# Norm 1 of a transformer block: shift and scale as fused sums over rows of 1024, squares summed on TensorE tile by tile

## The chip, the cores and the metric

The kernel runs on one core of one Trainium2 chip. A core has a matrix engine (TensorE, called PE in the profile, with its weight loads shown apart as PEld), a vector engine (VectorE, DVE), an engine for activations (ScalarE, ACT), a general one (GpSimd, POOL) and one that here only issues DMA transfers (SyncE, SP). Each engine has its own queue and takes its instructions in order; they wait for each other through semaphores. Data lie in SBUF, 128 partitions wide; TensorE writes its sums to banks of PSUM.

The metric is the device time of one execution, in microseconds, as the median of several runs.

## The reference, cut to what matters

One layer of an encoder block on 1024 tokens with 1024 channels. The change concerns only its first lines:

```python
c_act = jax.nn.silu(c)                              # c: 1 x 1024
mod = c_act @ ada_w[l] + ada_b[l]                   # 1024 x 6144 weights
sh1, sc1, g1, sh2, sc2, g2 = split(mod, 6)
h = rmsnorm(x, ln1_g[l]) * (1.0 + sc1) + sh1        # norm 1
p = h @ w_in[l]                                     # q, k, v, gates, convolution
```

`rmsnorm` divides every token by the root of the mean square of its 1024 channels and multiplies by `ln1_g`. Shift `sh1` and scale `sc1` are two vectors of 1024 numbers, each the product of the 1024 numbers silu(c) with a 1024 x 1024 part of `ada_w`. Everything after this (attention, convolution, gates, output projection, feed-forward network) is left as it is by the change.

## The kernel before

All is float32. Large products are done as three products of split operands: an operand is split into a rounded high part (`whi`, `hh`) and the rest (`wlo`, `hl`), and high x high, high x low and low x high are summed (lines 276 and 122 to 124).

The stage in question holds x transposed: 8 tiles of 128 channels by 1024 tokens (`xt`, 512 KB each). It does the following:

1. **Squares.** As each tile k arrives, ScalarE squares its two halves of 512 tokens (line 228) and VectorE adds them to a running sum `sqa` (line 230). TensorE multiplies each tile once by ones only to be warmed up (line 232). When all tiles are there, eight one-column products with `ones` sum `sqa` over the 128 channels of a tile, one for each 128 tokens, into columns of the PSUM tile `md` (line 234). Two small instructions (line 113, `rs_m`) and a power on GpSimd (line 114) give the inverse root, which TensorE spreads over all partitions (`bcast`, line 242).
2. **Shift and scale.** For each channel tile e, 1 MB of `ada_w` arrives as 128 partitions (input channels) by 8 input tiles by 256 outputs (128 of shift, 128 of scale). `mod_sums` (lines 201 and 204) does eight multiply-adds over 256 elements on VectorE: `acc` += `ada[:, k]` * silu(c) of partition and tile k. `mod_end` sums `acc` over the partitions by two one-column products with ones (line 214), adds the bias (line 215, `mod`) and forms (1 + scale) * gain (line 216, `a1`).
3. **h and the first product.** `norm_x` multiplies a half of an x tile by the inverse root (line 258, VectorE). `make_h` applies scale and shift (line 262, ScalarE), rounds (line 263, ScalarE) and takes the rest (line 264, GpSimd). `split_wq` splits half of a weight tile (lines 187, ScalarE, and 188, GpSimd). `real` then multiplies 7 of the 8 token tiles by 512 columns of the key/value weights: 21 products for each channel tile k (line 276). The eighth token tile follows where its PSUM bank is free.

The loop over k runs 7 times: VectorE does most of `mod_sums(k + 2)`, TensorE two or three token tiles, then `mod_end(k + 1)`, ScalarE and GpSimd make h(k + 1), and TensorE does the remaining token tiles. The order inside each engine is the order of the code: `in_order` ties every instruction of an engine to the one before it, from the squares to the end of this loop. Work from later in the program may be placed between by the planner, which orders the rest of the program by an estimate of its own. After the loop come the last channel tile, then the key products over the same h (loop over `cc`), whose weights are split by ScalarE and VectorE (lines 61 and 62), while GpSimd and VectorE form sums of parts of h (`factors`, line 127) for later products.

Transfers: x, then `ada` 0, weight 0, `ada` 1, 2, weight 1, `ada` 3 are queued on SP (lines 163, 170, 176); `ada` has two buffers that share the pool `big` with the squares and with h, and three of its own, so from tile 5 on a load waits for the sums of an earlier tile. Where h takes over a buffer of `ada`, GpSimd waits for its sums. Constants come by ScalarE's queue (line 97).

Of the kernel before, what the change touches and what calls it, by code (L numbers as in the profile page):

```python
# [8 lines left out]
F32 = mybir.dt.float32  # L9
F32R = mybir.dt.float32r  # L10
AF = mybir.ActivationFunctionType
ALU = mybir.AluOpType
# [4 lines left out]
P = 128  # L17
# [12 lines left out]
def block_kernel(tc, x, x_t, cols, ada_1, ada_2, ada_row, w_q, w_kv, w_v1, w_cg, w_a, w_b, w_o, w_g, w_u, w_d, out):  # L30
# [8 lines left out]
    def nm(s):  # L39
        uid[0] += 1  # L40
        return f"{s}_{uid[0]}"
# [119 lines left out]
    adb = bigp.tile([P, 2, KT, 256], F32, tag="big", bufs=4, name=nm("adb"))  # L161
    for k in range(KT):
        nc.sync.dma_start(xt[:, k, :], x_t[k])
    wq = []
    MC0, MC, MS, NS1, NM = 3, 2, 5, 2, 2
    ads = []

    def load_ada(e):
        ad = adb[:, e] if e < 2 else sp.tile([P, KT, 256], F32, tag="ada", bufs=3, name=nm("ada"))
        nc.sync.dma_start(ad, ada_1[e])  # L170
        ads.append(ad)

# [11 lines left out]
    def split_wq(k):  # L184
        cs = slice(k % 2 * 512, k % 2 * 512 + 512)
        hi, lo = wq[k // 2]
        nc.scalar.activation(hi[:, cs], wraw[k // 2][:, cs], AF.Copy)
        nc.gpsimd.tensor_tensor(out=lo[:, cs], in0=wraw[k // 2][:, cs], in1=hi[:, cs].bitcast(F32), op=ALU.subtract)
# [4 lines left out]
        load_ada(2 * q + 1)  # L193
    a1 = const.tile([P, 8], F32, name="a1")

    def mod_sums(e):

        ad = ads[e]
        acc = sp.tile([P, 256], F32, tag="acc", bufs=2, name=nm("acc"))
        accs[e] = acc  # L200
        nc.vector.tensor_scalar(out=acc, in0=ad[:, 0, :], scalar1=ca[:, 0:1], scalar2=None, op0=ALU.mult)
        yield
        for k in range(1, KT):
            nc.vector.scalar_tensor_tensor(out=acc, in0=ad[:, k, :], scalar=ca[:, k:k + 1], in1=acc,
                                           op0=ALU.mult, op1=ALU.add)
            yield

    accs = {}

    def mod_end(e):  # L210
        acc = accs.pop(e)
        ps = md[:, 2 * e:2 * e + 2]
        for j in range(2):
            nc.tensor.matmul(ps[:, j:j + 1], acc[:, j * P:(j + 1) * P], ones[:, 0:1], start=True, stop=True)
        nc.vector.tensor_tensor(out=mod[:, 0:2, e], in0=ps, in1=acol[:, 0:2, e], op=ALU.add)
        nc.vector.scalar_tensor_tensor(out=a1[:, e:e + 1], in0=mod[:, 1, e:e + 1], scalar=1.0,
                                       in1=ln1[:, e:e + 1], op0=ALU.add, op1=ALU.mult)


    sqa = sqb[:, 0]  # L220
    ssp = md[:, 16:24]
    rsp = [ps_tr() for n in range(2)]
    warm = ps_pj()
    for k in range(KT):
        for n in range(2):
            ns = slice(n * 512, n * 512 + 512)
            sq = sqb[:, 1 + k % 3, ns] if k else sqa[:, ns]
            nc.scalar.activation(sq, xt[:, k, ns], AF.Square)
            if k:
                nc.vector.tensor_tensor(out=sqa[:, ns], in0=sq, in1=sqa[:, ns], op=ALU.add)  # L230
        if k < NWARM:
            nc.tensor.matmul(warm, ones, xt[:, k, :512], start=True, stop=True)
    for i in range(8):
        nc.tensor.matmul(ssp[:, i:i + 1], sqa[:, i * P:(i + 1) * P], ones[:, 0:1], start=True, stop=True)
    ms0 = mod_sums(0)
    for j in range(NM):
        next(ms0)
    rts = [rstd_of(ssp[:, 4 * n:4 * n + 4], 1.0 / D, sp, 4, eng=nc.vector) for n in range(2)]

    def bcast(n):  # L240
        for i in range(4):
            nc.tensor.matmul(rsp[n][:, i * P:(i + 1) * P], rts[n][:, i:i + 1].broadcast_to([P, P]), ident,
                             start=True, stop=True)
# [12 lines left out]
    def norm_x(k, n):  # L256
        src = xt[:, k, n * 512:(n + 1) * 512]
        nc.vector.tensor_tensor(out=src, in0=src, in1=rs[:, n * 512:(n + 1) * 512] if k else rsp[n], op=ALU.mult)
# [16 lines left out]
                if q in parts:  # L275
                    nc.tensor.matmul(ps, a, b, start=(k == 0 and q == 0), stop=(k == KT - 1 and q == 2))  # L276

    for _ in ms0:
        pass
    def sums(k):  # L280
        ms = mod_sums(k)
        for j in range(8):
            next(ms)
            if j in (3, 5):
                norm_x(k, j // 4)
            yield

    split_wq(0)
    bcast(0)
    ms = sums(1)  # L290
    for j in range(NS1):
        next(ms)
    norm_x(0, 0)
    mod_end(0)
    bcast(1)
    norm_x(0, 1)
    make_h(0, 0)
    for n in range(2):
        nc.scalar.activation(rs[:, n * 512:(n + 1) * 512], rsp[n], AF.Copy)
    make_h(0, 1)  # L300
    NPRE = 7
    pss = [ps_pj() for i in range(5)] + [ps_tr() for i in range(2)]

# [2 lines left out]
            for i in range(i0, i1):  # L306
                mm_tok(pss[i], i, wq, k, k + 1, parts)

    for _ in ms:
        pass  # L310
    for k in range(KT - 1):
        if k + 2 < KT:
            ms = sums(k + 2)
            for j in range(MS):
                next(ms)
        mc = MC if k else MC0
        real(k, 0, mc)
        split_wq(k + 1)
        mod_end(k + 1)
        for n in range(2):  # L320
            make_h(k + 1, n)
        real(k, mc, NPRE)
        for _ in ms:
            pass
        if k + 4 < KT:
            load_ada(k + 4)
            if k % 2 == 0:
                load_wq(k // 2 + 2)
# [1021 lines left out]
```

## Time and profile before

| | us |
|---|---|
| median of 3 runs | 1945.4 |
| lowest and highest | 1941.25, 1946.02 |
| the profiled execution, its own time | 1945.62 |
| its span in the profile | 1943.8 |
| TensorE busy | 1853.6 |
| VectorE busy | 1462.3 |
| ScalarE busy | 864.6 |
| GpSimd busy | 673.7 |
| mean granted TensorE clock | 0.986 |

In the rows of the profile, a time is in microseconds from the start of the span unless marked; "x3" counts instructions that a row puts together; "out<-in" names the tiles written and read; what stands in brackets is the idle time of the engine before the row and the instruction that ended it. A row of waits gives the waiting instruction, the one waited for, the total, how often, and the longest. In the rows by stretch (start:end), the columns are the length, the busy time and number of instructions of each engine asked for, the clock granted to TensorE (1.00 is full), the mean busy share of the DMA engines, and GB/s. In rows of groups stand busy time in us, mean of one in ns, and the idle time before them. L204 is line 204 of the kernel.

### The profile page before, as it was taken

The numbers are of one execution on the slowest core, as the hardware profiler recorded it, in microseconds if no ns is written. First come the engines' busy times: TensorE is split into PE (matmuls) and PEld (weight loads), VectorE is DVE, ScalarE is ACT, GpSimd is POOL, SyncE is SP. The second block draws the span as 40 slices with busy tenths as digits, with TensorE's granted clock in tenths as the row PEclk, the third lists the DMA queues.
The fourth block names the chain that finished last, engine by engine and source line by source line (L and its number), as shares of the span: only waits on it lengthen the run. The fifth ranks groups of instructions, "written<-read, shape, count | busy, mean of one in ns | idle before, by whom it ended". The sixth has DMA issues, their size and how long they took to land.

```text
span 1943.8 us, 25154 instructions
## 1 busy us (share of the span) xinstructions
PE 1853.6 (95%) x8869; PEld 1519.5 (78%) x8869; DVE 1462.3 (75%) x1927; ACT 864.6 (44%) x1597; POOL 673.7 (35%) x475
## 2 busy tenths in 40 slices
PE   7899999998999999998999999979999999999899
PEld 4678767777888888887888788867888888878587
DVE  8865687778664799998999644499988788743854
ACT  4442343223333677776777421464444434422221
POOL 3694547978231001111000000065454444301713
PEclk8899999999999999999999999999999999999999
DMA  6465544334445756559554535323343334399566
GB/s 276 162 208 172 190 154 160 136 114 152 170 171 197 214 158 189 169 167 302 161 161 128 189 130 193 133 82 136 146 173 152 141 143 171 119 347 321 218 221 224
DMA packets 151149, 347.47 MB, mean 179 GB/s; under 512 B 15088, under 2 KB 52208, under 8 KB 149104
## 3 DMA queue, kind: packets, MB, share of 16 engines
q1 hardware_dynamic: 74000, 218.80, 34.4%
q10 hardware_dynamic: 76016, 123.40, 17.6%
q0 software_dynamic: 1008, 3.67, 0.5%
q8 instruction: 70, 1.15, 0.2%
q14 instruction: 55, 0.45, 0.1%
HBM read 235.19 MB, written 110.62 MB: 178 GB/s over the span
## 4 chain that ended last, share of the span: by engine, by line
PE 43%; DVE 10%; issue 3%; DMA 3%; ACT 2%; POOL 1%; ACTq 0%; SPq 0%; DVEq 0%; POOLq 0%
PE e L122 6%; PE e L124 6%; PE e L123 6%; PE e L1203 3%; PE e L1204 3%; PE e L1202 3%; PE pj L785 3%; PE pj L786 3%; PE pj L787 3%; DVE pt L710 2%; DVE wlo L965 2%; PE e L1020 1%; PE e L1022 1%; PE e L1021 1%; PE tr L726 1%
## 5 line engine op out<-in xcount | busy, mean ns | idle before, releaser
L710 DVE TENSOR_TENSOR_SCAN pt<-pt,dm 128x256 f32<-128x256 f32 (+7 forms) x128 | 173.9, 1363 | 5.3 <-ACT pt L705 5.1
L123 PE MATMUL e<-big,whi 128*128 128x512 f32 x352 | 138.0, 392 | 7.8 <-DVE big L127 7.8
L122 PE MATMUL e<-big,whi 128*128 128x512 f32 x352 | 137.7, 392 | 0.8 <-ACT c L1118 0.8
L124 PE MATMUL e<-big,wlo 128*128 128x512 f32 x352 | 137.5, 391 | 0.0
L1203 PE MATMUL e<-wlo,f 128*128 128x512 f32 (+1 forms) x319 | 123.1, 386 | 9.5 <-DVE wlo L965 9.5
L124 PE MATMUL pj<-big,wlo 128*128 128x512 f32 x320 | 127.0, 398 | 5.1 <-DVE wlo L127 5.1
L113 POOL TENSOR_SCALAR rs_m<-ss 128x1 f32<-128x1 f32 x8 | 2.0, 245 | 365.3 <-ACT xn L1035 365.3
L122 PE MATMUL pj<-big,whi 128*128 128x512 f32 x320 | 128.0, 400 | 0.4 <-ACT whi L438 0.4
L276 PE MATMUL pj<-whi,big 128*128 128x512 f32 x352 | 116.3, 410 | 11.6 <-ACT big L263 8.9
L123 PE MATMUL pj<-big,whi 128*128 128x512 f32 x320 | 127.1, 397 | 0.0
L705 ACT ACTIVATE pt<-z,rq 128x512 f32<-128x512 f32 (+2 forms) x192 | 112.3, 587 | 30.5 <-PE z L704 17.6
L1204 PE MATMUL e<-whi,f 128*128 128x512 f32 (+1 forms) x319 | 121.8, 382 | 0.0
L1202 PE MATMUL e<-whi,f 128*128 128x512 f32 (+1 forms) x319 | 118.5, 383 | 2.0 <-ACT fs L1142 1.4
L127 DVE TENSOR_TENSOR c<-e,c 128x512 f32<-128x512 f32 x154 | 102.8, 681 | 21.1 <-PE e L124 21.1
L829 POOL TENSOR_TENSOR ybl<-cy,ybh 128x512 fp32r<-128x512 f32 x16 | 29.0, 1810 | 255.7 <-ACT ybh L828 242.9
L438 ACT ACTIVATE whi<-raw 128x512 fp32r<-128x512 f32 x116 | 72.7, 633 | 94.4 <-PE pj L123 32.6
L706 ACT ACTIVATE sg<-z,rq 128x512 f32<-128x512 f32 (+1 forms) x192 | 112.7, 590 | 1.3 <-DVE mb L851 1.3
L127 DVE TENSOR_TENSOR c<-pj,c 128x512 f32<-128x512 f32 x140 | 93.2, 681 | 24.3 <-PE pj L124 24.1
L127 DVE TENSOR_TENSOR wlo<-ws,whi 128x512 fp32r<-128x512 f32 x80 | 73.6, 939 | 50.0 <-ACT whi L438 49.8
L730 DVE TENSOR_TENSOR atl<-tr,ath 128x512 fp32r<-128x512 f32 (+1 forms) x192 | 100.3, 544 | 10.7 <-ACT ath L729 10.3
L127 POOL TENSOR_TENSOR ws<-raw,raw 128x512 f32<-128x512 f32 x41 | 57.9, 1412 | 144.1 <-DMA raw<-w_cg 80.7
L729 ACT ACTIVATE ath<-tr 128x512 fp32r<-128x512 f32 (+1 forms) x192 | 90.4, 498 | 37.8 <-PE tr L726 12.7
(250 smaller groups left out, 5641.9 us busy)
## 6 DMA issues: line engine op xcount, KB each, us to landing
f<-d_f SPq DMA_DIRECT2D x77, 512.0 KB, 4.4
d_f<-fs ACTq DMA_DIRECT2D x70, 512.0 KB, 2.6
raw<-w_cg SPq DMA_DIRECT2D x40, 512.0 KB, 3.4
mada<-ada ACTq DMA_DIRECT2D x32, 512.0 KB, 4.2
raw<-w_g SPq DMA_DIRECT2D x24, 512.0 KB, 3.2
raw<-w_u SPq DMA_DIRECT2D x23, 512.0 KB, 3.2
d_k<-khl ACTq DMA_DIRECT2D x32, 256.0 KB, 2.2
d_q<-gt ACTq DMA_DIRECT2D x32, 256.0 KB, 2.1
```

The lines of the kernel that those rows point to most:

```text
L122: nc.tensor.matmul(ps, wh[:, k, :], fh[:, k, :], start=(k == 0), stop=False)
L123: nc.tensor.matmul(ps, wh[:, k, :], fl[:, k, :], start=False, stop=False)
L124: nc.tensor.matmul(ps, wl[:, k, :], fh[:, k, :], start=False, stop=(k == 3))
L127: eng.tensor_tensor(out=out, in0=a, in1=b, op=op)
L276: nc.tensor.matmul(ps, a, b, start=(k == 0 and q == 0), stop=(k == KT - 1 and q == 2))
L705: nc.scalar.activation(pt[:, off + s0:off + s0 + m], z[:, :m], AF.Sigmoid, scale=rq[:, 1, i, h:h + 1])
L706: nc.scalar.activation(sg[:, s0:s0 + m], z[:, :m], AF.Sigmoid, scale=rq[:, 0, i, h:h + 1])
L710: nc.vector.tensor_tensor_scan(out=pt[:, rev], data0=pt[:, rev], data1=dm[:, rev], initial=0.0, op0=ALU.mult, op1=ALU.add)
L730: nc.vector.tensor_tensor(out=tl[:, :nb, c0:c0 + P], in0=src, in1=th[:, :nb, c0:c0 + P].bitcast(F32), op=ALU.subtract)
L1202: nc.tensor.matmul(o, sh, w[0][:, c], start=(j == 0), stop=False)
L1203: nc.tensor.matmul(o, sh, w[1][:, c], start=False, stop=False)
L1204: nc.tensor.matmul(o, sl, w[0][:, c], start=False, stop=(j == NJ - 1))
```

## The change

Two things are done in another way, and the loop is reordered.

- **Squares:** ScalarE squares the first half of each x tile and VectorE the second; there is no running sum on VectorE. TensorE sums the squares of each tile as it comes: eight one-column products for every tile, accumulated in `md` over all 8 tiles (64 in place of 8).
- **Shift and scale:** `ada_w` is laid out the other way round, with 128 output channels on the partitions and 1024 inputs in a row, for shift and for scale. silu(c) is spread over all partitions: a 512 KB broadcast transfer of c on ScalarE's queue (`cab`), a sigmoid and a product, placed after the second tile of x. One fused instruction on VectorE then multiplies a row of 1024 by `cab` and sums it (`mod_sum`); two of them, for shift and for scale, replace the eight multiply-adds and the two one-column products. Each is issued as two instructions, the product and the read of the accumulator.
- **Order:** `mod_sum`, `mod_end` and `norm_x` of tile k + 2 now follow `make_h` of k + 1 in the code, in one piece, and no longer wait for TensorE. Before the loop, the sums of tile 0 come after the `rs_m` instructions, and those of tile 1 after the norm of tile 0.

```diff
+    cab = sp.tile([P, D], F32, name="cab")
+    nc.scalar.dma_start(cab, ada_row[2:3, :].broadcast_to([P, D]))
...
+    def mod_sum(e, m):
+        if not m:
+            msum[e] = sp.tile([P, 2], F32, tag="msum", bufs=4, name=nm("msum"))
+        pr = sp.tile([P, D], F32, tag="prod", bufs=2, name=nm("prod"))
+        nc.vector.tensor_tensor_reduce(out=pr, in0=ads[e][:, m], in1=cab, scale=1.0, scalar=0.0, op0=ALU.mult,
+                                       op1=ALU.add, accum_out=msum[e][:, m:m + 1])
...
     def mod_end(e):
-        acc = accs.pop(e)
-        ps = md[:, 2 * e:2 * e + 2]
-        for j in range(2):
-            nc.tensor.matmul(ps[:, j:j + 1], acc[:, j * P:(j + 1) * P], ones[:, 0:1], start=True, stop=True)
-        nc.vector.tensor_tensor(out=mod[:, 0:2, e], in0=ps, in1=acol[:, 0:2, e], op=ALU.add)
+        nc.vector.tensor_tensor(out=mod[:, 0:2, e], in0=msum.pop(e), in1=acol[:, 0:2, e], op=ALU.add)
...
     for k in range(KT):
-        for n in range(2):
-            ns = slice(n * 512, n * 512 + 512)
-            sq = sqb[:, 1 + k % 3, ns] if k else sqa[:, ns]
-            nc.scalar.activation(sq, xt[:, k, ns], AF.Square)
-            if k:
-                nc.vector.tensor_tensor(out=sqa[:, ns], in0=sq, in1=sqa[:, ns], op=ALU.add)
+        sq = sqb[:, k % 4]
+        nc.scalar.activation(sq[:, :512], xt[:, k, :512], AF.Square)
+        nc.vector.tensor_tensor(out=sq[:, 512:], in0=xt[:, k, 512:], in1=xt[:, k, 512:], op=ALU.mult)
         if k < NWARM:
             nc.tensor.matmul(warm, ones, xt[:, k, :512], start=True, stop=True)
-    for i in range(8):
-        nc.tensor.matmul(ssp[:, i:i + 1], sqa[:, i * P:(i + 1) * P], ones[:, 0:1], start=True, stop=True)
+        for i in range(8):
+            nc.tensor.matmul(ssp[:, i:i + 1], sq[:, i * P:(i + 1) * P], ones[:, 0:1], start=(k + i == 0), stop=(k + i == KT + 6))
+        if k == 1:
+            sb = sp.tile([P, D], F32, tag="prod", bufs=2, name=nm("sb"))
+            nc.scalar.activation(sb, cab, AF.Sigmoid)
+            nc.vector.tensor_tensor(out=cab, in0=cab, in1=sb, op=ALU.mult)
...
     for k in range(KT - 1):
-        if k + 2 < KT:
-            ms = sums(k + 2)
-            for j in range(MS):
-                next(ms)
         mc = MC if k else MC0
         real(k, 0, mc)
         split_wq(k + 1)
-        mod_end(k + 1)
         for n in range(2):
             make_h(k + 1, n)
+        if k + 2 < KT:
+            for m in range(2):
+                mod_sum(k + 2, m)
+            mod_end(k + 2)
+            for n in range(2):
+                norm_x(k + 2, n)
         real(k, mc, NPRE)
```

More of the change, by code (lines that the diff above doesn't have):

```diff
@@ L276, in mm_tok @@
                     nc.tensor.matmul(ps, a, b, start=(k == 0 and q == 0), stop=(k == KT - 1 and q == 2))
[L278 to L282, printed above, removed]
-            next(ms)
-            if j in (3, 5):
-                norm_x(k, j // 4)
-            yield
     split_wq(0)
+    for m in range(2):
+        mod_sum(0, m)
+    mod_end(0)
     bcast(0)
-    ms = sums(1)
-    for j in range(NS1):
-        next(ms)
     norm_x(0, 0)
-    mod_end(0)
     bcast(1)
+    make_h(0, 0)
     norm_x(0, 1)
-    make_h(0, 0)
+    make_h(0, 1)
     for n in range(2):
         nc.scalar.activation(rs[:, n * 512:(n + 1) * 512], rsp[n], AF.Copy)
-    make_h(0, 1)
+    for m in range(2):
+        mod_sum(1, m)
+    mod_end(1)
+    for n in range(2):
+        norm_x(1, n)
     NPRE = 7
```

33 lines of the change are left out of this document (8 added, 25 removed).

## The prediction

> **What bounds the kernel now.** I read the page first, then the waits of the first 110 us, one step of the loop in order of time, and the start in order of time. The diff touches only the work before the first key/value product is done; of everything later the changed program keeps the order, but for some local swaps. So the question is when that product ends.
>
> ```profile
> span 1943.8 us, 25154 instructions
> PE 1853.6 (95%) x8869; PEld 1519.5 (78%) x8869; DVE 1462.3 (75%) x1927; ACT 864.6 (44%) x1597; POOL 673.7 (35%) x475
> ```
> ```profile
> ACT xt L262 <- DVE a L216: 36.6, 8, 7.0
> ```
> ```profile
> 43.90:51.70 7.80, 5.75 (x27) 4.20 (x26) 7.62 (x13) 3.27 (x6) 4.15 (x4) 1.00 0.75 269
> ```
> Over the kernel TensorE (PE) is the bound, but not here. The waits say that ScalarE, whose `big` TensorE multiplies, waits for `a` of VectorE (36.6 us in 8 steps). The row of one loop step (columns: PE, PEld, DVE, ACT, POOL busy) has VectorE busy 7.62 of 7.80 us. One step, in order of time:
>
> ```profile
> 43.53 2.76 POOL L264 TENSOR_TENSOR big<-xt,big 128x512 fp32r<-128x512 f32 x2 [3.65 <-ACT big L263]
> 43.77 1.38 DVE L201 TENSOR_SCALAR acc<-ada,ca 128x256 f32<-128x256 f32 x1
> ...
> 45.19 3.33 DVE L204 SCALAR_TENSOR_TENSOR acc<-ada,ca,acc 128x256 f32<-128x256 f32 x3
> 46.25 1.46 POOL L188 TENSOR_TENSOR wlo<-raw,whi 128x512 fp32r<-128x512 f32 x1
> ...
> 48.43 0.68 DVE L258 TENSOR_TENSOR xt<-xt,rs 128x512 f32<-128x512 f32 x1
> 49.03 0.48 DVE L204 SCALAR_TENSOR_TENSOR acc<-ada,ca,acc 128x256 f32<-128x256 f32 x1
> 49.43 0.15 DVE L215 TENSOR_TENSOR mod<-pj,cst 128x2 f32<-128x2 f32 x1
> ...
> 49.81 0.81 ACT L262 ACTIVATE xt<-xt,mod,a 128x512 f32<-128x512 f32 x1 [4.47 <-DVE a L216]
> ...
> 51.36 2.76 POOL L264 TENSOR_TENSOR big<-xt,big 128x512 fp32r<-128x512 f32 x2 [3.65 <-ACT big L263]
> ```
> A multiply-add takes 0.48 us alone (49.03) and 1.11 on average beside GpSimd (3.33 for 3). Each GpSimd instruction is followed by one VectorE instruction, and so on: with inputs from SBUF they take turns. A step is therefore not the sum of VectorE's own work, but of the turns of both.
>
> **The start, and what the change adds to it.** All squares of x are now summed on TensorE as each of the 8 tiles arrives: per tile the warm-up product and 8 one-column products, each as two load-and-multiply pairs (16 rows for 8 products in the profile). Before, that was done once, after 14 adds on VectorE.
>
> ```profile
> 7.16 0.34 PEld L232 LDWEIGHTS pj<-xt,ones 128*128 128x128 f32 x1 [0.52 <-DMA xt<-x_t]
> 8.02 0.34 PEld L232 LDWEIGHTS pj<-xt,ones 128*128 128x128 f32 x1 [0.52 <-issue]
> ...
> 9.46 0.19 PEld L232 LDWEIGHTS pj<-xt,ones 128*128 128x128 f32 x1 [0.25 <-issue]
> 9.89 0.19 PEld L232 LDWEIGHTS pj<-xt,ones 128*128 128x128 f32 x1 [0.24 <-issue]
> ...
> 14.77 1.86 PEld L234 LDWEIGHTS pj<-ones,sqb 128*128 128x128 f32 x16 [1.15 <-DVE sqb L230]
> ...
> 20.92 0.93 PEld L214 LDWEIGHTS pj<-ones,acc 128*128 128x128 f32 x4 [1.61 <-DVE acc L204]
> 21.73 1.83 PEld L242 LDWEIGHTS tr<-dm,rs_r 128*128 128x128 f32 x8
> ```
> ```profile
> 4.47 9.98 PE L232 MATMUL pj<-xt,ones 128*128 128x512 f32 x16 [4.47 <-DMA xt<-x_t]
> ...
> 16.76 0.23 DVE L113 TENSOR_SCALAR rs_m<-pj 128x4 f32<-128x4 f32 x2 [0.16 <-PE pj L234]
> ...
> 24.08 1.65 PE L276 MATMUL pj<-whi,big 128*128 128x512 f32 x3 [0.23 <-ACT big L263]
> ```
> A pair starts every 0.11 us at the full clock (1.86 for 16) and every 0.21 at half clock (1.83 for 8, less the tail of the last; the 4 one-column pairs at 20.92 go at the same rate). One half of the warm-up product takes 0.86 us at the start (7.16 to 8.02) and 0.43 once the clock is full (9.46 to 9.89). So a tile costs 2 x 0.855 + 16 x 0.213 = 5.12 us at half clock; at full clock both terms halve, to 0.85 + 1.78 = 2.63. In both cases this is more than the 1.2 us in which a tile of x arrives (9.98 for 8), so TensorE sets the end of this stage. Which clock it gets decides the whole change:
>
> ```profile
> 16.01:19.42 3.41, 1.79 (x15) 1.00 1.04 438
> 19.42:22.83 3.41, 1.99 (x10) 0.50 1.01 423
> ...
> 50.14:53.56 3.42, 1.87 (x8) 1.00 0.48 134
> 53.56:56.97 3.41, 3.41 (x19) 1.00 0.92 257
> ...
> 60.38:63.79 3.41, 3.05 (x10) 0.50 0.48 204
> 63.79:67.21 3.42, 3.42 (x9) 0.50 0.44 153
> 67.21:70.60 3.39, 3.39 (x18) 1.00 0.00 0
> ```
> ```profile
> 60.75 1.22 PE L276 MATMUL pj<-whi,big 128*128 128x512 f32 x2 [0.36 <-POOL big L264]
> 61.77 0.85 PE L214 MATMUL pj<-ones,acc 128*128 128x1 f32 x4
> 62.48 1.63 PE L276 MATMUL pj<-whi,big 128*128 128x512 f32 x3
> ```
> These are stretches of TensorE (busy us, count, granted clock), cut where the clock changes, every 3.41 us. The stretch from 60.38 is busy for 3.05 of 3.41 us and the next one is still at half clock; only after 63.79 to 67.21, all of it wide products, is the clock full. What the first lacks is columns: five products of 512 columns at some 0.43 us (1.63 for 3, less the tail of the last) are 2.1 us, 62%; the four one-column pairs fill time but stream nothing. In the same way 1.79 us of narrow work (from 16.01) loses the clock and 1.87 us of mostly wide work (from 50.14) keeps it. In the new start the streaming share is 1.71 of 5.12 us, and at most 1.71 of any 3.41, 50%. So I take half clock to the end of the stage: 4.47 + 8 x 5.12 = 45.4, and `rs_m` at 45.6 in place of 16.76: **+28.8 us**.
>
> The Trainium skill's page TensorE: Matmul & The Clock Gate (section Why this matters for your kernels) advises to keep TensorE busy for at least 4 us without a gap to get the full clock. Taken by queue occupancy, that rule would let this stage run at full clock, for the result of the second rival below; the 60.38 row does not agree with it so read.
>
> Hidden in this stage: the second half of each square, moved to VectorE (8 x 0.68 in place of 14 adds); the sigmoid and the product for `cab` (about 1.6 us on ScalarE, twice the 0.81 of a pass over 512, and as much on VectorE); the 512 KB broadcast, issued on ScalarE's queue ahead of its squares, which takes x's transfers some 1.2 us at the 420 to 440 GB/s of the rows above. Their cover is TensorE's 5.1 us a tile; without it they cost at most their own time. SP's queue keeps its order; the five `ada` tiles that have a buffer, with x and three weights some 11 MB, need 26 us at that rate and are there. The later three wait for a sum to free a buffer, as before, and have three steps to land.
>
> **The loop.** Removed per step: 8 multiply-add instructions and 4 one-column pairs with the wait of `mod` for TensorE. Added: 2 fused sums over 1024 with a read of the accumulator each. No row has this instruction. Bounds, by nearest rows of 1024 elements from SBUF:
>
> ```profile
> L710 DVE TENSOR_TENSOR_SCAN pt<-pt,dm 128x1024 f32<-128x1024 f32 x16 | 36.5, 2279 | 0.6 <-ACT pt L705 0.5
> ...
> L712 DVE TENSOR_TENSOR sg<-sg,pt 128x1024 f32<-128x1024 f32 x16 | 19.8, 1240 | 0.1
> ```
> ```profile
> 29.34 1.27 POOL L264 TENSOR_TENSOR big<-xt,big 128x512 fp32r<-128x512 f32 x1 [3.97 <-DVE acc L204]
> ```
> The plain product, 1.24 us, is the lower end (it must stream the same elements); the scan, 2.28, the upper, since it also carries a value along the row. A sum needs no value for each element before the next product, so I take 1.24, plus 0.1 for the read (the small `mod` above takes 0.15, overlapped).
>
> The Trainium skill's Vector Engine (DVE) Microarchitecture Reference (section 7, Points that are easy to get wrong) says that two-source instructions with accumulator run at half rate when both sources are SBUF and wider than bf16. That would be the upper end, and the first rival's result; no row here shows such an instruction, only that the multiply-add without accumulator does not (256 elements in 0.48).
>
> Turns per step: GpSimd 3 x 1.27 = 3.8; VectorE 2 x 1.1 + 2 x 0.53 (the streaming parts of 1.24 and 0.68) = 3.3; together **7.1 us** in place of 7.85 (43.53 to the like place at 51.36). VectorE's own work, 4.3 us, would allow less, but turns are taken in order. `mod` and `a` now both have two sources in SBUF and wait for a turn; they are short and fall between.
>
> From `rs_m`: itself 0.2, two sums 2.7, a turn of GpSimd 1.3, `mod` and `a` 0.3, the norm 0.7, ScalarE's two passes 0.8 + 0.6: first product at +6.7 (before: 24.08 - 16.76 = 7.3). Step 0 runs at half clock for most of its 24 products at 0.427 and takes 8; then 6 steps of 7.1; the last h at +57.
>
> ```profile
> 84.90:95.80 10.90, 10.90 (x49) 1.00 0.38 118
> ```
> ```profile
> 85.10 6.01 POOL L127 TENSOR_TENSOR tb<-big,big 128x512 f32<-128x512 f32 x4
> ```
> Then TensorE alone: 39 products at 0.227 us (this row: 10.9 for 48 or so), 8.9 us: the product ends at +65.8. Before, it ended at 95.85 (the last of its 192 products is at the end of that row), 79.1 after `rs_m`. Gain **-13.3**. The eighth token tile may start early, as the bank `md` is free; that moves 7 of its 24 products into TensorE's gaps and is in the 39.
>
> After it, the fourth weight of the next product is split on VectorE behind two factor instructions that need six GpSimd instructions after the last `hl`. At 1.5 us each (6.01 for 4) or a little more these end near +69, the split near +71; TensorE wants it at 65.8 + 18 x 0.227 = +69.9. I take **+1** (bounds 0 and 2.5); before, GpSimd's last `hl` was 10.7 us ahead of the product's end (85.10), now some 7.
>
> Sum: 28.8 - 13.3 + 1 = +16.5 on 1945.6, the profiled execution's own time (its span 1943.8 and 1.8 around it), 0.2 above the median: **1962**.
>
> **Rivals.**
> 1. The fused sum costs 2.28 us. That is 2.1 us more per step, 16.6 in 8 steps: the product ends at +82.4, 3.3 later than before counted from `rs_m`; 28.8 + 3.3 + 1 = +33: 1978.5. For it: the scan's row. Against: see above.
> 2. Not slower: TensorE's clock counts loads too and goes full at about 9.2 us, where it did before. Then 7.1 tiles at 2.63 us, `rs_m` at 28: +11.2 - 13.3 + 1 = -1: 1944.5. It decides at the first tiles: their pairs at 0.11 in place of 0.21. For it: TensorE never idles. Against: the 60.38 row.
> 3. The fused sum does not take turns with GpSimd. Then the loop is TensorE's own: 192 products in 43.6 us and some 3 for half clock, the end at +53.3, gain 25.8; 28.8 - 25.8 + 1 = +4: 1949.5. Against: the multiply-adds at 45.19, whose sources are in SBUF too, stretch beside GpSimd.
> 4. Rivals 1 and 2 together: 1961.
>
> **Numbers.** Forecast 0.66 (1955 to 1967, from 0.6 us a tile and 0.3 us a step), rival 1 0.13, rival 2 0.12, rival 3 0.05, rival 4 0.04. The range 1948 to 1981 leaves out rival 2. About 0.3% (6 us) is what a measurement can tell from no change: slower 0.84, same 0.12, faster 0.04 (rival 2 with a cheaper start).
>
> **What would show it.** One-column pairs 0.21 us apart and clock 0.50 up to 40 us or so; `rs_m` near 45; fused sums of 1.2 to 1.3 us where GpSimd rests, longer beside it; steps of 7 us; no wait of `mod` for TensorE. Pairs 0.11 apart, or sums above 2 us alone, make it wrong.

## The result, and the profile after

The changed kernel takes 1966.3 us (median of 5 runs, 1964.18 to 1971.89) against 1945.4 us (1941.25 to 1946.02): a ratio of 1.0115 (95% interval 1.010 to 1.013). The profiled execution took 1964.18 us, its span 1962.4.

VectorE is busy for 1452.8 us, 10 less than before, and TensorE for 1874.8, 21 more; over the whole span that says little. The three places that matter follow.

**The start.** TensorE in order of time, then the instruction that ends the stage, then one tile as a stretch (busy us and count of each engine, granted clock, DMA share, GB/s). In the changed kernel the warm-up product is L222 and the one-column products are L224.

```profile
4.63 2.05 PE L222 MATMUL pj<-xt,ones 128*128 128x512 f32 x2 [4.63 <-DMA xt<-x_t]
6.46 3.41 PE L224 MATMUL pj<-ones,sqb 128*128 128x1 f32 x16
9.74 2.06 PE L222 MATMUL pj<-xt,ones 128*128 128x512 f32 x2
...
42.31 3.41 PE L224 MATMUL pj<-ones,sqb 128*128 128x1 f32 x16
```
```profile
45.76 0.23 DVE L113 TENSOR_SCALAR rs_m<-pj 128x4 f32<-128x4 f32 x2 [19.79 <-PE pj L224]
45.90 1.22 DVE L203 CUSTOM_DVE_ANT_0 prod<-adb,cab 128x1024 f32<-128x1024 f32 x1
47.04 0.08 DVE L203 DVE_READ_ACCUMULATOR2_ANT msum<- 128x1 f32 x1
```
```profile
14.86:19.98 5.12, 5.12 (x20) 4.09 (x20) 1.62 (x3) 0.67 (x2) 0.00 (x0) 1.00 1.02 427
```

From 4.63 to 9.74 is one tile, 5.11 us; 16 pairs take 3.41 us, 0.213 each, in the last tile as in the first. TensorE is busy for all 5.12 us of a tile and still runs at half rate (why the clock column reads 1.00 here is told with the 128-column run). VectorE waits 19.8 us for it. The fused sum (L203, shown as a custom instruction) takes 1.22 us with nothing beside it, and the read of its accumulator 0.08.

**A step of the loop**, in order of time:

```profile
80.09 0.81 ACT L253 ACTIVATE xt<-xt,mod,a 128x512 f32<-128x512 f32 x1 [3.63 <-DVE xt L249]
...
81.64 3.54 POOL L255 TENSOR_TENSOR big<-xt,big 128x512 fp32r<-128x512 f32 x2 [2.21 <-ACT big L254]
...
81.73 2.31 DVE L203 CUSTOM_DVE_ANT_0 prod<-ada,cab 128x1024 f32<-128x1024 f32 x1
...
84.08 1.13 DVE L209 TENSOR_TENSOR mod<-msum,cst 128x2 f32<-128x2 f32 x1
85.15 1.28 POOL L190 TENSOR_TENSOR wlo<-raw,whi 128x512 fp32r<-128x512 f32 x1
85.24 1.21 DVE L210 SCALAR_TENSOR_TENSOR a<-mod,cst 128x1 f32<-128x1 f32 x1
...
87.09 0.81 ACT L253 ACTIVATE xt<-xt,mod,a 128x512 f32<-128x512 f32 x1 [3.63 <-DVE xt L249]
```

80.09 to 87.09: 7.00 us a step. Beside GpSimd the second fused sum takes 2.31 us, and `mod` and `a`, a few elements each, take 1.13 and 1.21: each waits for the GpSimd instruction that runs just then.

**The end of the product.** The product's own instructions (line L267; L276 before), cut where its 192nd one is done; the first fence is of before, the second of after. The columns are TensorE's busy time, count, clock, DMA share and rate.

```profile
16.00:95.84 79.84, 56.04 (x192) 0.85 0.51 189
95.84:192.20 96.36, 91.20 (x385) 1.00 0.59 187
```
```profile
45.00:115.85 70.85, 50.62 (x192) 0.95 0.38 137
115.85:215.95 100.10, 93.19 (x385) 0.97 0.58 180
```

So the product ends 79.1 us after `rs_m` before and 70.1 after. Against the terms of the prediction, in the two profiled executions:

| Term | predicted | measured |
|---|---|---|
| `rs_m` (16.76 to 45.76) | +28.8 | +29.0 |
| from `rs_m` to the end of the product (79.1 to 70.1) | -13.3 | -9.0 |
| the next two products (96.3 to 100.1, starts of the 192nd and the 576th) | +1 | +3.8 |
| everything later | 0 | -5.2 |
| span | +16.5 | +18.6 |

The total is close, but the last three terms are each off by 3 to 5 us, and these misses nearly cancel. The profiled execution of the changed kernel was the fastest of its five; by the medians the change costs 20.9 us, not 18.6.

### The profile page after: what moved, and what is told of

It is laid out like the page before. It is cut to its first block, busy times and chain, and to the rows that moved or that the text cites. A ratio compares the mean times of both kernels' runs of the same rounds, so it can differ in the third digit from the quotient of the medians.

```text
span 1962.4 us, 25269 instructions
## 1 busy us (share of the span) xinstructions
PE 1874.8 (96%) x8949; PEld 1540.2 (78%) x8949; DVE 1452.8 (74%) x1890; ACT 861.2 (44%) x1590; POOL 678.3 (35%) x475
## 4 chain that ended last, share of the span: by engine, by line
PE 59%; DVE 18%; POOL 8%; issue 6%; DMA 5%; ACT 3%; ACTq 0%; SPq 0%; DVEq 0%; POOLq 0%
PE e L123 6%; PE e L122 6%; PE e L124 6%; DVE pt L692 4%; PE pj L267 4%; PE e L1185 3%; PE e L1186 3%; PE e L1184 3%; PE pj L767 3%; PE pj L768 3%; PE pj L769 3%; PE pj L122 3%; PE pj L124 3%; PE pj L123 2%; POOL ws L127 2%
## 5 line engine op out<-in xcount | busy, mean ns | idle before, releaser
L687 ACT ACTIVATE pt<-z,rq 128x512 f32<-128x512 f32 (+2 forms) x192 | 112.5, 588 | 30.8 <-PE z L686 17.8
L267 PE MATMUL pj<-whi,big 128*128 128x512 f32 x352 | 114.1, 407 | 11.9 <-ACT big L254 10.0
L127 DVE TENSOR_TENSOR c<-e,c 128x512 f32<-128x512 f32 x154 | 103.0, 682 | 22.7 <-PE e L124 22.5
```

What stands on the lines that cost most here:

```text
L127: eng.tensor_tensor(out=out, in0=a, in1=b, op=op)
L687: nc.scalar.activation(pt[:, off + s0:off + s0 + m], z[:, :m], AF.Sigmoid, scale=rq[:, 1, i, h:h + 1])
```

## The experiments

Times are medians; ratios are against the kernel before on the same chip, with 95% intervals. "Last" is the start of the 192nd instruction of the first key/value product.

| Kernel | us | ratio to before | `rs_m` | last |
|---|---|---|---|---|
| before | 1945.4 | 1 | 16.76 | 95.6 |
| after | 1966.3 | 1.0115 (1.010 to 1.013) | 45.76 | 115.6 |
| start only | 1974.3 | 1.0163 (1.0148 to 1.0178) | 45.66 | 122.2 |
| loop only, early `cab` | 1945.6 | 1.0015 (1.0004 to 1.0025) | 24.28 | 94.0 |
| loop only, late `cab` | 1938.8 | 0.999 (0.9973 to 1.0007) | 18.58 | 86.5 |
| no warm-up products | 1957.5 | 1.0072 (1.0054 to 1.0091) | 33.9 | 104.1 |
| 128 columns | 1947.3 | 1.0015 (1.0001 to 1.0029) | 28.1 | 97.6 |
| squares as moving rows | 1949.4 | 1.0024 (1.001 to 1.0038) | 27.0 | 97.6 |
| no GpSimd in the loop | 1958.6 | 1.0077 (1.0051 to 1.0102) | 45.7 | 106.5 |
| `mod`, `a` with one tensor | 1962.5 | 1.0104 (1.0079 to 1.0129) | 45.6 | 112.2 |
| four factor adds moved | 1968.0 | 1.013 (1.0101 to 1.0158) | 45.6 | 116.7 |
| factors asked for later | 1968.9 | 1.014 (1.011 to 1.017) | 45.6 | 114.2 |
| weight splits held back | 1966.1 | 1.0139 (1.0116 to 1.0161) | 46.0 | 116.0 |
| loop only, late `cab`, no GpSimd | 1928.2 | 0.993 (0.9905 to 0.9954) | 18.4 | 82.1 |

### The two halves of the change

Start only: the kernel before with the new sum of squares.

```diff
-            sq = sqb[:, 1 + k % 3, ns] if k else sqa[:, ns]
-            nc.scalar.activation(sq, xt[:, k, ns], AF.Square)
-            if k:
-                nc.vector.tensor_tensor(out=sqa[:, ns], in0=sq, in1=sqa[:, ns], op=ALU.add)
+        sq = sqb[:, k % 4]
+        nc.scalar.activation(sq[:, :512], xt[:, k, :512], AF.Square)
+        nc.vector.tensor_tensor(out=sq[:, 512:], in0=xt[:, k, 512:], in1=xt[:, k, 512:], op=ALU.mult)
...
+        for i in range(8):
+            nc.tensor.matmul(ssp[:, i:i + 1], sq[:, i * P:(i + 1) * P], ones[:, 0:1], start=(k + i == 0), stop=(k + i == KT + 6))
```

> The kernel before with the squares summed on TensorE tile by tile, 64 one-column products, and its loop unchanged: the start's part of the change alone. Theory: tiles 5.12 us apart at half clock, rs_m at 45.7 in place of 16.76, the whole later program moved by 28.9: 1974 (1971 to 1976). Rival (part of the lost time is cover for loads that the loop before waits for): 1966 or less.

1974.3: in the theory's range; against the kernel before on the same chip (1943.4) it is 30.8 more. `rs_m` comes at 45.66, and the 192nd instruction of the product starts 76.6 after it, 2.3 sooner than the 78.9 of before. So next to nothing of the lost 29 us comes back.

Loop only: the changed kernel with the old sum of squares, and the sigmoid for `cab` left behind the second tile.

```diff
-        sq = sqb[:, k % 4]
-        nc.scalar.activation(sq[:, :512], xt[:, k, :512], AF.Square)
-        nc.vector.tensor_tensor(out=sq[:, 512:], in0=xt[:, k, 512:], in1=xt[:, k, 512:], op=ALU.mult)
+        for n in range(2):
+            ns = slice(n * 512, n * 512 + 512)
+            sq = sqb[:, 1 + k % 3, ns] if k else sqa[:, ns]
+            nc.scalar.activation(sq, xt[:, k, ns], AF.Square)
+            if k:
+                nc.vector.tensor_tensor(out=sqa[:, ns], in0=sq, in1=sqa[:, ns], op=ALU.add)
...
+    for i in range(8):
+        nc.tensor.matmul(ssp[:, i:i + 1], sqa[:, i * P:(i + 1) * P], ones[:, 0:1], start=True, stop=True)
```

> The changed kernel with the squares summed as before (14 adds on VectorE, then 8 one-column products once), and the fused sums kept: the loop's part of the change alone. Theory (start and loop are two separate terms: the start costs 28.8, the loop gains): rs_m near 17 in place of 45.8, loop steps of 7.0 us, and the first key/value product ends some 70 us after rs_m as it does in the changed kernel, near 87 against 95.85 before. That is 9 us sooner; GpSimd's rope factors, which start later against the product, give up to 4 back: about 1938 (1935 to 1942), faster than both kernels. Rival (the late start also gave the loop something, say its loads, so that the loop alone gains nothing): 1945.

1945.6: the rival's number, but not by the rival's mechanism. The 192nd instruction of the product starts 69.7 us after `rs_m`, as in the changed kernel (69.9); what is late is `rs_m`, 24.28 in place of 16.76. ScalarE, TensorE and VectorE, in order of time:

```profile
11.68 1.06 ACT L229 ACTIVATE sb<-cab 128x1024 f32<-128x1024 f32 x1 [4.54 <-DMA cab<-ada_row]
12.64 6.33 ACT L222 ACTIVATE sqb<-xt 128x512 f32<-128x512 f32 x12
...
20.67 3.57 PE L232 MATMUL pj<-ones,sqb 128*128 128x1 f32 x16 [4.62 <-DVE sqb L224]
...
24.28 0.23 DVE L113 TENSOR_SCALAR rs_m<-pj 128x4 f32<-128x4 f32 x2 [3.06 <-PE pj L232]
```

ScalarE stands at the sigmoid for 4.54 us because the broadcast row, issued at 4.54, lands 7.1 us later, between the fifth and the sixth tile of x, and 12 of the 16 squares are queued behind it. The one-column products that sum the squares then run at half rate, 3.57 us in place of 1.95: that is 1.6 of the 7.5 us. In the changed kernel the same wait (5.4 us in the waits) is hidden by TensorE's 5.1 us a tile. So the sigmoid was put behind the last square:

```diff
-        if k == 1:
+        if k == KT - 1:
             sb = sp.tile([P, D], F32, tag="prod", bufs=2, name=nm("sb"))
```

> The first experiment (squares summed as before, fused sums kept) with the sigmoid and the product for cab put behind the last square instead of behind the second. In the first experiment ScalarE's squares waited 4.5 us there for the broadcast row to land, and rs_m came at 24.3 in place of 16.8. Theory (that wait, and nothing in the loop, took the gain): rs_m at 17, the first key/value product 70 us later at 87, the total 7.3 under the first experiment: 1938 (1936 to 1941), faster than both kernels. Rival (the loop, without the late start, waits for its loads): rs_m at 17 but the product after 90, 1942 or more.

1938.8, 6.8 under the early form (4.9 by the two ratios). `rs_m` comes at 18.58 (the product for `cab`, 1.22 us, now stands right ahead of it on VectorE) and the last product 67.9 later. "Faster than both kernels" can't be claimed from its interval, which just reaches 1.

### The clock in the first stage

Without the warm-up products:

```diff
-        if k < NWARM:
-            nc.tensor.matmul(warm, ones, xt[:, k, :512], start=True, stop=True)
```

> The changed kernel without the 8 warm-up products in the first stage (they compute nothing that is used). Theory (a tile is 2 x 0.855 for the warm-up product plus 16 x 0.213 for the pairs, nothing else bounds it): tiles 3.41 us apart, still at half clock since the pairs stream one column each, rs_m near 32.0, the total 13.7 us under the changed kernel: 1952.6 (1950 to 1955). Rival (the squares or the transfers bound a tile): tiles stay above 4.5 us, 1960 or more. Rival (the clock counts pairs as activity and the warm-up products hinder nothing): the clock goes full and rs_m comes before 22: 1942.

`rs_m` at 33.9. TensorE over the whole stage:

```profile
5.67 6.99 PE L221 MATMUL pj<-ones,sqb 128*128 128x1 f32 x32 [5.67 <-ACT sqb L218]
13.26 20.64 PE L221 MATMUL pj<-ones,sqb 128*128 128x1 f32 x96 [0.60 <-ACT sqb L218]
```

A pair still takes 0.215 us, so the 5.12 is the sum of the two parts, and with nothing but pairs the rate stays half. The stage is 1.9 later than forecast: pairs now start only when the first square is there (5.67), and 0.6 goes to a wait for a square (13.26). The total fell by 9, not by 13.7; the first product kept 11.5 of it.

The same 64 products and loads, but 128 columns wide:

```diff
-            nc.tensor.matmul(ssp[:, i:i + 1], sq[:, i * P:(i + 1) * P], ones[:, 0:1], start=(k + i == 0), stop=(k + i == KT + 6))
+            nc.tensor.matmul(rsp[i // 4][:, i % 4 * P:(i % 4 + 1) * P], sq[:, i * P:(i + 1) * P], ones, start=(k == 0 and i % 4 == 0), stop=(k == KT - 1 and i % 4 == 3))
...
```

> The changed kernel with each one-column product widened to 128 equal columns: the same 64 products, the same weight loads, 128 times the columns streamed (column 0 of each is read). Theory (the clock follows the columns streamed, not the loads, and a load runs beside the product ahead of it): the first tile takes the same 5.1 us at half clock, then the clock is full from the second or third stretch of 3.41 us on and a tile takes 2.6: rs_m at 27 to 31, the total near 1950 (1947 to 1954), though each product does more. Rival (something else holds the clock down, or the clock counts occupancy): clock 0.50 to the end of the stage, tiles of 5.1 us or more, 1966 or more. Rival (load and product add up, so that a tile takes 8.5 at half clock and the streaming share is 60%): rs_m near 73, 1993.

```profile
6.34 3.62 PE L223 MATMUL tr<-ones,sqb 128*128 128x128 f32 x16
9.75 1.07 PE L221 MATMUL pj<-xt,ones 128*128 128x512 f32 x2
10.65 1.95 PE L223 MATMUL tr<-ones,sqb 128*128 128x128 f32 x16
```

The first tile takes the same 3.4 us for its pairs; from the second on it is 1.8 and the warm-up product half as long: full clock, to the end of the stage. `rs_m` is 17.7 us earlier although each product streams 128 times as much. TensorE is busy in both kernels (here but for one gap of 0.2 us) and the loads are the same; what differs is the columns. The traces' own records of the clock agree: the first one, of full clock, begins at 9.8 us here, at 51.7 in the changed kernel, at 40.0 without the warm-up products and at 9.2 in the kernel before. Before its first record the clock column reads 1.00 whatever the rate, and the durations tell. That columns raise the clock is the step on which the prediction hung, and it is shown here.

Squares as the moving operand, two products of 512 columns a tile, and the columns picked by eight fused sums with the identity:

```diff
-        for i in range(8):
-            nc.tensor.matmul(ssp[:, i:i + 1], sq[:, i * P:(i + 1) * P], ones[:, 0:1], start=(k + i == 0), stop=(k + i == KT + 6))
+        for n in range(2):
+            nc.tensor.matmul(rsp[n], inv_d, sq[:, n * 512:n * 512 + 512], start=(k == 0), stop=(k == KT - 1))
...
```

> The changed kernel with the squares as the moving operand: per tile 2 products of 512 columns against a constant matrix of 1/1024 (squares written rounded for the single-pass product), summed in two banks; eight fused multiply-and-sums of 128 columns with the identity then pick the columns for rs_m. Theory (streamed columns raise the clock; a tile is 1.71 + 2 x 0.43 = 2.56 at half clock and 1.28 at full, next to the 1.25 in which it arrives): the clock is full from about 10 us, the last product near 17, rs_m near 19, the first key/value product some 8 us sooner than before, the total near 1940 (1937 to 1944). Rival (the clock stays at half for another reason): the last product near 25, 1947 or more.

```profile
9.67 1.02 PE L223 MATMUL pj<-xt,ones 128*128 128x512 f32 x2
13.60 0.79 PE L225 MATMUL tr<-sqb,inv_d 128*128 128x512 f32 x1 [2.90 <-ACT sqb L220]
...
15.53 1.91 PE L223 MATMUL pj<-xt,ones 128*128 128x512 f32 x2
...
20.29 1.02 PE L223 MATMUL pj<-xt,ones 128*128 128x512 f32 x2
```

A miss by 9 us. The clock does go full by 9.67, but ScalarE's wait for `cab` (5.7 us here) then leaves TensorE idle for 2.9 us, and from 15.53 the products are at half rate again until 20.29. With a fast TensorE the hidden wait is no longer hidden: the cause of the loop-only run once more.

### The loop

GpSimd's three subtractions of a step on VectorE, from the second step on:

```diff
-        nc.gpsimd.tensor_tensor(out=hl[n][:, k, :], in0=src, in1=hh[n][:, k, :].bitcast(F32), op=ALU.subtract)
+        if not k:
+            make_hl(nc.gpsimd, k, n)
...
+            mod_sum(k + 2, 0)
+        make_hl(nc.vector, k + 1, 0)
+        split_lo(k + 1)
+        if k + 2 < KT:
+            mod_sum(k + 2, 1)
+        make_hl(nc.vector, k + 1, 1)
```

> The changed kernel with GpSimd's three subtractions of each loop step (two hl, one weight part) on VectorE, from the second step on. Theory (the step is the sum of the turns of GpSimd, 3 x 1.2, and of VectorE's streaming): the turns go, VectorE has 2 x 1.15 + 5 x 0.6 + 0.25 = 5.6 us a step, TensorE 5.45: steps of 5.7 in place of 7.0, six to seven of them, 8 to 9 us in all: 1958 (1955 to 1961). Rival (VectorE's instructions are long for another reason than GpSimd, or the chain through ScalarE sets the step): steps of 7 or more, 1966 or more.

```profile
74.56 0.82 ACT L259 ACTIVATE xt<-xt,mod,a 128x512 f32<-128x512 f32 x1 [2.19 <-DVE xt L255]
80.13 0.82 ACT L259 ACTIVATE xt<-xt,mod,a 128x512 f32<-128x512 f32 x1 [2.20 <-DVE xt L255]
...
96.05 1.06 ACT L61 ACTIVATE whi<-raw 128x1024 fp32r<-128x1024 f32 x1 [5.20 <-DMA raw<-w_kv]
```

5.57 us a step where all three moved, against 7.00: VectorE does more and the loop is shorter. The turns are shown. In the last two steps some of it is lost: a split of the next product's weights (L61) stands on ScalarE ahead of the pass and waits for its transfer, 2.1 us in the first of them and 5.2 in the second; these steps take 7.4 and 9.5.

`mod` and `a` with the second operand as a scalar per row:

```diff
-        nc.vector.tensor_tensor(out=mod[:, 0:2, e], in0=msum.pop(e), in1=acol[:, 0:2, e], op=ALU.add)
+        for m in range(2):
+            nc.vector.tensor_scalar(out=mod[:, m, e:e + 1], in0=ms[:, m:m + 1], scalar1=acol[:, m, e:e + 1], scalar2=None, op0=ALU.add)
...
```

> The changed kernel with mod and a computed by three small instructions that take their second operand as a scalar per row, so that each reads one tensor only. In the changed kernel mod waits 1.13 and a 1.21 us of a step, each for a turn of GpSimd. Theory (the step is the sum of all turns; who waits does not matter): mod and a take 0.15 to 0.2 each, the norm waits instead, steps stay at 7.0 us: 1966 (1964 to 1968). Rival (the two waits lie on the chain and go): 2 us a step, 1952.

```profile
83.16 0.33 DVE L211 TENSOR_SCALAR mod<-msum,cst 128x1 f32<-128x1 f32 x2
83.53 0.21 DVE L212 TENSOR_SCALAR a<-mod,cst 128x1 f32<-128x1 f32 x1
83.66 2.98 DVE L250 TENSOR_TENSOR xt<-xt,rs 128x512 f32<-128x512 f32 x2
```

The small instructions no longer wait, and the norm does: 2.98 us for two in place of 1.28. Steps are now 5.7 and 7.9 us in turn, 6.8 over a pair, against 7.0. So of the 1.8 us that `mod` and `a` no longer wait, only 0.2 leaves the step: who waits matters little, as the theory has it, and the rival's 2 us a step is out. But the product ended 3.4 us sooner (112.2 against 115.6), 1.3 of it ahead of the last step and most of the rest behind it, and that the theory did not expect. The total can't be told from the changed kernel's, the intervals overlap. The Trainium skill's page SBUF — State Buffer (section SBUF: two separate sides) has an exclusive lock that a VectorE instruction takes against GpSimd when both its inputs are in SBUF; these rows agree: 1.13 and 1.21 us with two tensors, 0.33 for two and 0.21 with one.

The last step of the loop takes 8.2 us in the changed kernel. The planner had put two splits of the next product's weights into it; they were held back, in the order of ScalarE and VectorE, behind the loop's last instruction there (`lasts`):

```diff
+    def hold(j0):
+        for i in nc.cur_bb.bb.instructions[j0:]:
+            if i.engine in lasts and i.engine in (nc.vector.engine, nc.scalar.engine):
+                tc.add_manual_dep(i, lasts[i.engine].name,
...
+        if cc == 1:
+            hold(j0)
```

> The changed kernel with the splits of the next product's first weights held back on ScalarE and VectorE until the loop's own work is issued. In the changed kernel the planner puts one of them on VectorE ahead of the last mod and a (2.31 us at 97.94), another between the last two ScalarE passes (1.04 us at 104.33). Theory (they, not the turns, make the last step 8.2 us and its second half 2.2 us late): the last step takes 7.0 as the others, TensorE gets the last h near 103.5 in place of 105.9, has no stretch at half clock there, and the first product ends near 112.5 in place of 115.9: 1963 (1960 to 1965). Rival (the splits are wanted by then: the next product waits for its weights and the gain is given back): 1965 to 1969.

The step did become 7.0 us (94.33 to 101.31) and the last `hh` came at 103.5 in place of 105.3. The product ended no earlier. TensorE, then two stretches:

```profile
104.20 0.79 PE L267 MATMUL tr<-whi,big 128*128 128x512 f32 x1 [2.83 <-ACT big L254]
```
```profile
104.30:107.60 3.30, 3.17 (x7) 2.07 (x8) 2.47 (x2) 3.17 (x4) 3.22 (x2) 0.50 0.00 0
107.60:111.00 3.40, 3.40 (x10) 2.69 (x9) 3.40 (x3) 0.60 (x1) 3.40 (x3) 0.54 0.75 219
```

TensorE waits 2.8 us for the last h, loses the clock for two stretches, and needs 12 us for the last 38 products. The gain was given back to the clock.

### After the product

Four adds of the first group of rope factors on VectorE:

```diff
-                    tt(nc.gpsimd, b[e][n], hh[n][:, 4 * e + j, :].bitcast(F32), hl[n][:, 4 * e + j, :].bitcast(F32), ALU.add)
+                    tt(nc.vector if j == 0 else nc.gpsimd, b[e][n], hh[n][:, 4 * e + j, :].bitcast(F32), hl[n][:, 4 * e + j, :].bitcast(F32), ALU.add)
```

> The changed kernel with the first four adds of the rope factors on VectorE instead of GpSimd (5.0 us of GpSimd's work just after the last hl, while VectorE rests about half of the time). Theory (after the product it is GpSimd's queue that the key norms wait for, since GpSimd now starts the factors 8 us before the product ends and not 10.7): GpSimd is some 5 us ahead, TensorE's wait of 3.8 us near 134 shrinks by 3 or more: 1962.5 (1961 to 1964). Rival (the wait near 134 is VectorE's, which the move makes worse): 1966 to 1970.

```profile
123.05 7.91 POOL L127 TENSOR_TENSOR tb<-tb,tb 128x512 f32<-128x512 f32 x4
...
140.90 0.66 PE L364 MATMUL tr<-dm,qn 128*128 128x128 f32 x4 [3.20 <-DVE qn L358]
```

No gain. GpSimd has four instructions fewer, but the rest take up to 1.98 us each (7.91 for 4, in place of 1.5), and TensorE's wait for the key norm is still 3.2 us. It did not cost the clock here: the products after it start 0.23 us apart, as at full clock.

The factors' pieces asked for more slowly:

```diff
-            for _ in range(2 if cc else 0):
+            for _ in range((0, 1, 2)[cc]):
                 next(ml, None)
```

> The changed kernel with the rope factors' pieces asked for at one per tile in place of two during the first product with key norms. Theory (TensorE's wait of 4.2 us near 134 ends with a key norm that waits in GpSimd's queue behind the factors, 1.65 us for rs_r alone after three factor instructions; the wait is long enough to cost the clock as well): the norm comes earlier, the wait falls under 2 us, 1963.5 (1961 to 1965). Rival (the wait is only moved: the factors finish later and TensorE waits for them): 1966 to 1969.

This told nothing: on GpSimd the planner kept the order of the changed kernel, TensorE's wait is again 3.8 us, and the time is 1968.9. What would remove this wait stays open.

### The best version

The old squares, the fused sums, `cab` behind the last square, and no GpSimd in the loop, put together from the edits above:

```diff
-        if k == 1:
+        if k == KT - 1:
...
-        nc.gpsimd.tensor_tensor(out=hl[n][:, k, :], in0=src, in1=hh[n][:, k, :].bitcast(F32), op=ALU.subtract)
+        if not k:
+            make_hl(nc.gpsimd, k, n)
```

> The same with GpSimd's three subtractions of each loop step on VectorE from the second step on. Theory (the two gains add): steps of 5.6 us in place of 7.0, some 8 us off: 1930.5 (1927 to 1934). Rival (the loads of weights and modulation tables, 11 MB in all, can't keep up with an earlier and shorter loop): waits for transfers in the loop, steps above 6 us, 1934 or more.

1928.2 us, 0.7% under the kernel before (0.46 to 0.95%), and some 1.8% under the changed one by the two ratios (0.993 to 1.0115). Steps of 5.57 us; the last two again take 7.3 and 9.5.

## Why the prediction was right, and where only its sum was

**The start: right, step by step.** Tiles of 5.12 us, pairs of 0.213, `rs_m` at 45.76 against 45.6. The reason given, that columns and not loads or occupancy raise the clock, is shown by the run with 128 columns. The rule of the Trainium skill's page TensorE: Matmul & The Clock Gate (section Why this matters for your kernels), read by occupancy as the prediction set it against the trace, does not hold here: a tile is busy 5.12 of 5.12 us and stays at half rate. That run also makes the second rival's condition true: it put `rs_m` at 28 and the time at 1944.5; measured were 28.1 and 1947.3. Only the sign announced, a clock of 0.50 up to 40 us, can't be read: the trace has no record of the clock before 51.7 us. The durations, and that first record itself, take its place.

**The fused sum: right.** 1.22 plus 0.08, against 1.24 plus 0.1, so the first and the fourth rival fall. The Trainium skill's Vector Engine (DVE) Microarchitecture Reference (section 7, Points that are easy to get wrong) has half the throughput for one form of two-source instruction when both sources are in SBUF and not bf16, as no read port is left for the accumulator. The fused sum's 1.22 us for 1024 elements, no more than the plain product's 1.24, shows no such loss; the trace names it as a custom instruction, so that the page's form itself was not measured. The third rival falls by the 2.31 us beside GpSimd.

**The steps: right, with wrong details.** The first product came at `rs_m` + 6.7 as forecast, but in part by luck. The turn of GpSimd in that sum (1.3) did not come, `mod` and `a` were done by 48.7; the norm then waited about as long for something that the sum does not have, TensorE's spreading of the inverse root (L233):

```profile
50.20 0.69 DVE L249 TENSOR_TENSOR xt<-xt,tr 128x512 f32<-128x512 f32 x1 [1.53 <-PE tr L233]
```

Four of the seven steps took 7.00 against 7.1. That `mod` and `a` "fall between" the turns was wrong, they wait 1.1 to 1.2 us each; that this costs the step next to nothing was right, 0.2 us by their own experiment.

**The last part of the loop: wrong by 4.3 us.** The step that failed is "Then TensorE alone: 39 products at 0.227 us, 8.9". The last step's first product came at `rs_m` + 58.0, 1.1 late (the sum has 65.8 - 8.9 = 56.9); but the 39 products from there took 12.1 us:

```profile
103.77 0.50 PE L267 MATMUL pj<-whi,big 128*128 128x512 f32 x1 [2.63 <-ACT big L254]
...
105.94 0.50 PE L267 MATMUL tr<-whi,big 128*128 128x512 f32 x1 [1.44 <-ACT big L254]
```
```profile
108.15:111.60 3.45, 3.45 (x14) 2.73 (x13) 1.50 (x3) 1.58 (x3) 3.45 (x3) 0.77 0.34 126
```

TensorE waits twice for the halves of the last h and loses the clock. The prediction had a clock loss for step 0 (it took 7.2, not 8) and none here. The run with the splits held back shows that a wait for the last h is enough for the loss, without the splits.

**After the product: +3.8 for +1.** The step that was mis-sized is the term for GpSimd's end coming closer to TensorE's. Its place was wrong too: the fourth weight is 0.17 us late, but TensorE then waits 3.8 us for a key norm (and 3.4 us of the clock follow at half rate, as the row below shows), with `rs_r` on GpSimd behind factors.

```profile
132.89 1.29 POOL L127 TENSOR_TENSOR tb<-tb,tb 128x512 f32<-128x512 f32 x1
134.14 1.72 POOL L127 TENSOR_TENSOR tb<-big,big 128x512 f32<-128x512 f32 x1
135.81 1.65 POOL L114 TENSOR_TENSOR rs_r<-rs_m,nhalf 128x8 f32<-128x8 f32 x1
138.24 1.11 PE L364 MATMUL tr<-dm,qn 128*128 128x128 f32 x4 [3.83 <-DVE qn L358]
138.88:142.30 3.42, 3.42 (x11) 2.74 (x10) 0.00 (x0) 0.00 (x0) 3.25 (x4) 0.50 0.43 162
```

Over these two products TensorE is idle for 2.1 us before and 3.8 after, and after, ten products start some 0.43 us apart, before one: the wait and the half rate are about one half of the +3.8 each. The rows show what the norm stands behind: `rs_m` of the key norm is done at 132.81, and two factor instructions run on GpSimd ahead of `rs_r`. That another order would shorten the time was not shown: in both experiments on it two factor instructions still stood there.

**Later: -5.2 for 0.** The prediction took the rest to be moved as a whole. From the start of the 576th instruction of the product to the end of the span, the 14 profiled executions of these kernels, with the same code there but for what the planner moves, took 1744.4 to 1755.2 us; the kernel before took 1751.9 and the changed one 1746.7. So -5.2 is no more than such executions differ by, and that it made up for other misses is luck. The largest piece is one idle spell of TensorE, which ScalarE ends after a wait for a transfer. Before (first two fences) and after (last two):

```profile
920.14 1.25 ACT L729 ACTIVATE ath<-tr 128x512 fp32r<-128x512 f32 x3 [7.37 <-DMA sqt<-d_q]
920.79 0.58 PE L741 MATMUL o<-ath,vt 128*128 128x256 f32 x1 [4.40 <-ACT ath L729]
```
```profile
920.54:924.00 3.46, 3.06 (x13) 2.77 (x14) 3.22 (x5) 3.46 (x8) 0.00 (x0) 0.50 0.99 308
924.00:927.30 3.30, 3.30 (x15) 3.11 (x14) 2.48 (x5) 1.99 (x6) 0.00 (x0) 0.50 0.60 212
```
```profile
940.75 1.26 ACT L711 ACTIVATE ath<-tr 128x512 fp32r<-128x512 f32 x3 [5.29 <-DMA sqt<-d_q]
941.40 0.38 PE L723 MATMUL o<-ath,vt 128*128 128x256 f32 x1 [2.33 <-ACT ath L711]
```
```profile
942.60:946.00 3.40, 3.40 (x19) 3.40 (x17) 3.30 (x6) 2.89 (x6) 0.00 (x0) 0.50 1.03 329
946.00:949.40 3.40, 3.40 (x22) 2.97 (x21) 2.89 (x4) 2.10 (x5) 0.00 (x0) 1.00 0.87 332
```

TensorE is idle for 4.40 us before and 2.33 after, which brings the two traces from 22.7 to 20.6 us apart. Then two stretches are at half clock before and only one after, which brings them to 19.5. Why the transfer was awaited for less, and the other 2.0 us, were not followed up. The Trainium skill's TensorE: Matmul & The Clock Gate (section What's actually happening) says that the clock's window runs freely and does not start with the kernel. The traces agree: the recorded changes lie on a grid of 3.41 us that begins 2.36 us after the start of the span before and 0.49 us after it in the changed kernel.

So the span's +18.6 was met within 2.1 us by +16.5, with two right terms and three misses that nearly cancel; the median, 1966.3, lies 4.3 above the forecast and inside its range.

## What to carry to other kernels

Before moving a reduction to TensorE, count the columns that it streams in 3.4 us: here products of one column left it at half rate though it was busy all the time, and the same products 128 columns wide were done 17.7 us sooner. Where VectorE and GpSimd both read SBUF, count a loop in turns of both: here, taking work off GpSimd and giving it to the busier VectorE made the step 1.4 us shorter. A wait that is hidden under a slow engine can come back as soon as that engine is made faster; ask of each covered transfer which engine's queue stands behind it.

## What was not expected of the hardware

- TensorE stayed at half rate for the whole first stage of the changed kernel, 41 us, without a pause: every pair takes 0.213 us and every warm-up half 0.86, twice the durations at full clock, and the first record of full clock begins at 51.7.
- A hidden 512 KB broadcast does not cost "at most its own time" once its cover is gone: it cost 7.5 us of `rs_m` (24.28 against 16.76), since it landed 7 us after its issue, the squares were queued behind the instruction that waits for it, and TensorE summed them at half rate (1.6 of the 7.5 us).
- An idle spell of 2.6 to 2.9 us of TensorE cost the clock in the changed kernel (2.63, with 1.44 more close behind), with the splits held back (2.83) and in the run with moving squares (2.90). One of 3.2 us in the run with four factor adds moved did not. What decides was not measured.
